# Keys kept on chip, three output products moved into the attention's order, and row sums taken later, in one step of a hybrid decoder

## The chip, the cores and the metric

The kernel runs on one core of a Trainium2 chip. A core has a matrix engine (TensorE, PE in the profile, with its weight loads as PEld), a vector engine (VectorE, DVE), an activation engine (ScalarE, ACT), a general engine (GpSimd, POOL) and a queue engine (SyncE, SP) that issues transfers. SBUF is the on-chip memory, PSUM the eight banks into which TensorE accumulates, and DRAM the memory off the core. The metric is the device time of one execution in microseconds, the median of three runs.

## The reference

One decoder layer is computed for 1024 prompt rows and for 8 sequences with 4 new rows each, 1056 rows in all, with the same weights and a model width of 1024:

```python
h = rmsnorm(x, g_norm1) * (1 + scale1) + shift1
za, zq, zkv, zg, zm = split(h @ w_in)
u, v = split(gelu(za)); ya = chunk_spatial_gating(u, layernorm(v), w_spatial, b_spatial)
yb = nsa_attention(q, kv_rows, win_rows, ...)     # compressed + selected blocks + window, gated
gate_a, gate_b = split(sigmoid(zm))
x = x + gate1 * ((gate_a * (ya @ w_branch_a) + gate_b * (yb @ w_branch_b)) @ w_out)
up = (rmsnorm(x, g_norm2) * (1 + scale2) + shift2) @ w_up
a, gv = split(causal_conv(up)); x = x + gate2 * ((gelu(a) * gv) @ w_down)
y = rmsnorm(x, g_final)
```

The prompt attends to its own 16 blocks of 64 keys and to a window of 512. The 8 sequences have 8192 past rows in a paged cache: all pages are read once for the compressed keys, and once more for the selected-block branch, in which blocks that were not selected are masked. The keys of the new rows are an output too.

## The kernel before

All activations lie with features on the 128 partitions and the 1056 rows along the free axis. A matrix product in float32 is made of three products: every operand x is split into hi (rounded to the type fp32r, by ScalarE) and lo (the rest, by VectorE), and hi*hi, hi*lo and lo*hi are summed in PSUM (split, L319 and L320; products, L415). Rows are taken in three chunks, 384, 384 and 288 wide (CH). Wide tiles of 1056 come from one pool of 24 slots (slot).

The order of the instructions on an engine is found by a planner at build time, which simulates the program with its own costs and takes what is ready, the earliest written first. A tile's memory is taken when its first user is planned and given back after its last. With issue_after, a program edge keeps one instruction behind another on its engine; the argument behind of products and of down is a list of (step, instruction): from that step on, the matmuls stay behind that instruction. In the attention stage the order of TensorE alone is written by hand (manual_schedule); the other engines are still planned.

The stages that the change touches, in order:

*The dense stage.* A list fill (L813) holds 22 dense products of h with w_in: four queries, two keys, sixteen merge gates, each stored to DRAM when done. Between them lie the compressions of the paged cache (compress, compress_act, compress_end), one per half sequence; the last two, n = 14 and 15, come after fill. key(j) (L731) evacuates one key head pair, copies the new rows' part and stores the rest to the output o_k. hh and hl, the split h, hold 16 of the 24 slots until the last dense product is through.

*Key tiles and queries.* key_tiles(j) (L837) loads a key tile back from o_k and makes four tiles: hi and lo for each of two heads, with the 64 partitions of the head copied to the other 64 as well. queries (L854) splits the queries of one tile of 128 rows; the queries are loaded back from DRAM (L871).

*Attention.* There are 32 units (8 tiles of 128 prompt rows, taken in the order 4, 5, 1, 6, 0, 7, 2, 3, by 4 heads of a group). step(n) makes the scores of unit n, turns the probabilities of unit n - 1 and multiplies the values of unit n - 2. Among these it deals out 32 paged steps (sel_step) that read the pages of the 8 sequences, 2 MB each, through a ring of four buffers (page_buffer), which the modulation weights, the sequences' window and at the end ya and w_ba use too. due tells before which unit how many paged steps should be done; it goes by work, the keys that a unit sees plus a constant:

```python
work = [i + 1 + min(i + 1, 5) + 6 for i, _ in units]
```

Chains of small operations (masks, the merge of paged steps) are generators in a list pending: each call of one_more counts down their waits and runs what is due, and a yield of k says that the next part comes k calls later. blocks(gr, bank) (L749) is such a chain: it makes the compressed branch and the block mask of four sequences. After the last unit, the remaining ones run one after the other.

*Branch outputs.* The eight outputs of ya @ w_branch_a are made after the attention's PSUM banks were given back, each in three chunks with a gate tile that is loaded from DRAM (L1355) and multiplied in when the bank is evacuated (L1358). Then come those of w_branch_b (L1368 loads the weights), w_out, and the up-projection.

*Down-projection.* Per chunk, eight outputs m of 22 steps each; the residual is added (residual), the squares of x are summed over m (squares, L1422), and at the chunk's end rstd_rows (L274) sums over the partitions with matmuls of one column (m1 is the last), makes the reciprocal root with small operations, and broadcasts it back with transposes (m2 is the last). Both are placed within the next chunk's products by behind. y_tile then scales the outputs and stores them.

## Time and profile before

| | |
|---|---|
| median of 3 runs | 1963.92 us (1961.31 to 1966.83) |
| the profiled execution's own time | 1964.85 us |
| its span, first to last instruction | 1963.0 us |
| mean granted TensorE clock | 0.977 |
| TensorE busy | 1847.5 us, 94% |
| VectorE, ScalarE, GpSimd busy | 60%, 40%, 24% |

Times are in us from the start of the span. In the groups, a row reads: line, engine, operation, out<-in with shapes, count, busy time, mean of one, and the idle time before them with what ended it. In a timeline a row begins with its start and its length; a last bracket holds the idle time before it and what ended it. SPq is the SP queue's own issuing. A matmul's end is modelled. A granted clock of 1.00 is TensorE's full clock. The stages lie thus: dense products until about 587, compressions 14 and 15 until about 602, attention from 609 to 1011, the w_branch_a products to about 1061, the rest of the mixer and the up-projection after it, and the down-projection from about 1716 on; the last row sums are at 1946.

### The profile page before, as it was taken

Reading aid. Unit: us, or ns where it says so; the run is one execution under the profiler, and the core shown is the slowest. Engines: PE = TensorE matmul, PEld = TensorE weight load, DVE = VectorE, ACT = ScalarE, POOL = GpSimd, SP = SyncE. Lnnn points to the kernel's source line nnn. Section 1 sums busy time; section 2 is a strip of 40 time slices with the busy share of each in tenths; the row PEclk is TensorE's granted clock in tenths of the full one; section 3 lists DMA queues with packets and bytes.
Section 4 is the critical chain, followed back from the end, with each engine's and each line's share of the span. In section 5 each row is a group of like instructions: output and inputs, shape, how many; then the busy total and the mean of one; then the engine's idle time right before and its main releaser. Section 6 shows DMA issues by size and latency. Waiting matters only on the chain.

```text
span 1963.0 us, 43697 instructions
## 1 busy us (share of the span) xinstructions
PE 1847.5 (94%) x16031; PEld 1740.0 (89%) x16031; DVE 1178.8 (60%) x2554; ACT 785.6 (40%) x1602; POOL 465.8 (24%) x613
## 2 busy tenths in 40 slices
PE   5899999999997998989989999899999999999996
PEld 3799999999996776757679998899999999999996
DVE  7615311111116666666665778989999999756464
ACT  4313111122114554646642356434444444545342
POOL 2410100100000000000001411567867675201010
PEclk9899999999998999989999999999999999999998
DMA  8445657775748677777774454233322223956462
GB/s 329 152 153 165 203 163 227 242 225 184 227 164 274 191 223 236 226 236 220 235 251 152 140 165 152 71 105 105 109 88 73 83 78 95 309 180 207 136 190 88
DMA packets 253893, 346.13 MB, mean 176 GB/s; under 512 B 35280, under 2 KB 189296, under 8 KB 251504
## 3 DMA queue, kind: packets, MB, share of 16 engines
q1 hardware_dynamic: 205696, 262.91, 42.5%
q10 hardware_dynamic: 36896, 41.22, 6.7%
q0 software_dynamic: 11088, 39.21, 5.6%
q8 instruction: 127, 2.08, 0.4%
q14 instruction: 86, 0.70, 0.1%
HBM read 305.96 MB, written 41.43 MB: 177 GB/s over the span
## 4 chain that ended last, share of the span: by engine, by line
PE 77%; DVE 6%; SPq 5%; DMA 5%; issue 3%; ACT 2%; DVEq 0%; ACTq 0%
PE t L56 75%; SPq L522 4%; DMA t<-w_ada 2%; PE t L1161 2%; DVE t L320 1%; DMA t<-t 1%; SPq L512 1%; ACT t L319 1%; DVE t L1135 1%; DMA t<-psel 1%; ACT t L1136 1%; ACT t L1165 1%; DMA t<-pcmp 0%; DVE t L338 0%; DMA t<-w_rows 0%
## 5 line engine op out<-in xcount | busy, mean ns | idle before, releaser
L56 PE MATMUL t<-t,t 128*128 128x264 f32 (+11 forms) x15256 | 1772.7, 305 | 84.7 <-DVE t L173 14.8
L56 PEld LDWEIGHTS t<-t,t 128*128 128x128 f32 (+2 forms) x15096 | 1658.6, 170 | 137.8 <-issue 61.6
L320 DVE TENSOR_TENSOR t<-t,t 128x512 fp32r<-128x512 f32 (+2 forms) x478 | 390.7, 825 | 317.7 <-ACT t L319 295.7
L319 ACT CAST t<-t 128x512 fp32r<-128x512 f32 (+5 forms) x544 | 310.5, 588 | 422.8 <-PE t L56 322.2
L1584 DVE TENSOR_TENSOR t<-t,t 128x264 f32<-128x264 f32 (+2 forms) x366 | 107.4, 339 | 12.8 <-PE t L56 12.8
L1192 POOL COPY t<-t 128x256 f32<-128x256 f32 x32 | 13.2, 412 | 298.9 <-DVE t L1190 190.8
L1161 PEld LDWEIGHTS t<-t,t 128*128 128x128 f32 x528 | 57.3, 142 | 29.2 <-ACT t L1010 9.2
L1521 ACT ACTIVATE t<-t,t 128x1072 f32<-128x1072 f32 x44 | 56.6, 1286 | 64.8 <-DVE t L1584 39.8
L1522 DVE SCALAR_TENSOR_TENSOR t<-t,t,t 128x1072 f32<-128x1072 f32 x44 | 71.6, 1627 | 10.7 <-ACT t L1521 10.1
L683 ACT ACTIVATE t<-t 128x384 f32<-128x384 f32 (+1 forms) x48 | 22.2, 465 | 138.6 <-PE t L56 89.1
L1136 ACT ACTIVATE t<-t,t 128x640 f32<-128x640 f32 (+3 forms) x64 | 56.2, 879 | 48.0 <-DVE t L1135 42.0
L1165 ACT COPY t<-t 128x512 f32<-128x512 f32 (+1 forms) x112 | 58.6, 567 | 40.4 <-PE t L1161 40.3
L1161 PE MATMUL t<-t,t 128*128 128x128 f32 x528 | 73.6, 278 | 0.7 <-DVE t L1213 0.3
L1135 DVE TENSOR_REDUCE t<-t 128x1 f32<-128x640 f32 (+3 forms) x64 | 58.9, 922 | 19.9 <-PE t L56 18.2
L1713 POOL TENSOR_TENSOR t<-t,t 128x384 f32<-128x384 f32 (+1 forms) x12 | 14.9, 1274 | 229.3 <-ACT t L1771 229.3
L1523 DVE SCALAR_TENSOR_TENSOR t<-t,t,t 128x1072 f32<-128x1072 f32 x44 | 63.2, 1435 | 0.0
L685 POOL DMA_DIRECT2D t<-t x16 | 8.5, 534 | 219.7 <-DVE t L684 165.0
L1547 POOL TENSOR_TENSOR t<-t,t 128x512 f32<-128x512 f32 x21 | 35.4, 1687 | 105.0 <-DMA t<-w_up 67.3
L1615 POOL TENSOR_TENSOR t<-t,t 128x1024 f32<-128x1024 f32 x22 | 54.3, 2469 | 17.1 <-ACT t L1614 17.1
L981 DVE TENSOR_TENSOR t<-t,t 128x512 f32<-128x512 f32 x32 | 22.1, 690 | 41.2 <-PE t L56 41.0
L1402 POOL TENSOR_TENSOR t<-t,t 128x384 f32<-128x384 f32 (+1 forms) x24 | 27.9, 1168 | 71.8 <-DVE t L1401 68.6
L320 DVE TENSOR_TENSOR t<-t 128x384 fp32r<-128x384 f32 (+1 forms) x66 | 36.2, 576 | 13.3 <-ACT t L319 13.2
(285 smaller groups left out, 1272.3 us busy)
## 6 DMA issues: line engine op xcount, KB each, us to landing
t<-psel SPq DMA_DIRECT2D x512, 128.0 KB
t<-pcmp SPq DMA_DIRECT2D x332, 128.0 KB
t<-w_down SPq DMA_DIRECT2D x120, 256.0 KB
t<-t POOLq DMA_DIRECT2D x50, 528.0 KB, 4.3
t<-w_up SPq DMA_DIRECT2D x96, 256.0 KB
t<-pcmp ACTq DMA_DIRECT2D x180, 128.0 KB
t<-w_ada SPq DMA_DIRECT2D x16, 1024.0 KB
t<-w_t ACTq DMA_DIRECT2D x52, 256.0 KB
```

What stands on the lines that cost most here:

```text
L56: return pe.matmul(out, lhsT, rhs, start=start, stop=stop)
L319: act.copy(hi, t)
L320: dve.tensor_tensor(lo, t, hi.bitcast(F32), op=OP.subtract)
L522: d = queue.dma_start(dst, src[bass.ds(r, 1)].rearrange("g p c -> p (g c)"))
L1135: dve.tensor_reduce(m4[:, branch, h:h + 1], ps[:, :, 0:w], axis=AX.XY, op=OP.max, negate=True)
L1136: act.activation(P[:, 0:L].rearrange("p (a c) -> p a c", a=2), ps[:, :, 0:w], AF.Exp, bias=m4[:, branch, h:h + 1], accum_out=s4[:, branch, ...
L1161: pe.transpose(pt[:, c:c + 128], probs[branch, h][:, 128 * b:128 * b + 128], ident)
L1165: (act.copy if w > 2 else dve.tensor_copy)(probs[branch, h][:, 128 * k:128 * (k + w)], pt[:, c:c + 128 * w])
L1521: act.activation(acc[:, 0:w], up[:, 0:w], AF.Identity, scale=cw[:, n, 0:1], bias=cw[:, n, 3:4])
L1522: dve.scalar_tensor_tensor(acc[:, 0:w], up[:, 1:1 + w], cw[:, n, 1:2], acc[:, 0:w], op0=OP.mult, op1=OP.add)
L1523: dve.scalar_tensor_tensor(acc[:, 0:w], up[:, 2:2 + w], cw[:, n, 2:3], acc[:, 0:w], op0=OP.mult, op1=OP.add)
L1584: dve.tensor_tensor(o, by4(banks[c][:, c0:c0 + n], n), other(c, c0, n) if other else o, op=OP.add)
```

## The change

- Both keys go to the end of fill, and key keeps its tile in kr_of. key_tiles reads this tile in place of loading o_k, and is called ahead of the query loads. The copy of k to the other 64 partitions is made by ScalarE from the key itself, not by VectorE from the rounded one. The queries of the first tile are split between compressions 14 and 15.
- In blocks the second yield is 6, not 3.
- The constant in work is 1, not 6.
- The loop body of the w_branch_a outputs becomes branch_a(m, bank). Outputs 0, 1 and 2 run inside the hand-written order, with the attention's banks (pM), and three calls of one_more after each chunk; outputs 3 to 7 run where all eight ran. products gets the argument bank.
- In the down-projection, m1 is asked for at step 12 of the next chunk's first output, not 4, and m2 at step 2 of its second output, not step 14 of the first.
- In the last chunk the last square isn't added to the sum by VectorE; the row sums take both tiles.

```diff
-    def products(w, xh, xl, a, b, evac, behind=()):
-        ps = pA()[:, 0:b - a]
+    def products(w, xh, xl, a, b, evac, behind=(), bank=pA):
+        ps = bank()[:, 0:b - a]
...
+    kr_of = []
     def key(j):
         kr = slot()
+        kr_of.append(kr)
...
-        yield 3
+        yield 6
         pt = bank()
...
-    fill = [lambda j=j: query(j) for j in range(4)] + [lambda j=j: key(j) for j in range(2)]
-    fill += [lambda j=j: merge_gate(j, slot()) for j in range(16)]
+    fill = [lambda j=j: query(j) for j in range(4)] + [lambda j=j: merge_gate(j, slot()) for j in range(16)]
+    fill += [lambda j=j: key(j) for j in range(2)]
...
-    def key_tiles(j, anchor):
+    def key_tiles(j):
...
-        kr = slot()
-        if anchor is not None:
-            dve.tensor_copy(kr[0:1, 0:1], anchor[0:1, R - 1:R])
-        sync.dma_start(kr[:, 0:NP], A["o_k"][j][:, 0:NP])
-        f = kr[:, 0:NP]
+        f = kr_of[j][:, 0:NP]
         for h, k, l in ((0, k0, l0), (1, k1, l1)):
             own, other = slice(64 * h, 64 * h + 64), slice(64 - 64 * h, 128 - 64 * h)
             act.copy(k[own, 0:NP], f[own])
+            act.copy(k[other, 0:NP], f[own])
             dve.tensor_tensor(l[own, 0:NP], f[own], k[own, 0:NP].bitcast(F32), op=OP.subtract)
-            dve.tensor_copy(k[other, 0:NP], k[own, 0:NP].bitcast(F32))
             dve.tensor_copy(l[other, 0:NP], l[own, 0:NP].bitcast(F32))
...
+    key_tiles(0)
+    key_tiles(1)
     qt = [slot() for _ in range(4)]
     for j in range(4):
         sync.dma_start(qt[j], q_d[j])
-    key_tiles(0, None)
-    key_tiles(1, None)
...
+    compress_act(*compress(14))
     q_first = queries(TILES[0], KL[0][0])
-    for n in (14, 15):
-        compress_act(*compress(n))
+    compress_act(*compress(15))
     compress_end()
...
-    work = [i + 1 + min(i + 1, 5) + 6 for i, _ in units]
+    work = [i + 1 + min(i + 1, 5) + 1 for i, _ in units]
...
         for n in range(len(units) + AHEAD):
             step(n)
+        ma = []
+
+        def branch_a(m, bank):
+            w = slot(F32R)
+            split(wba[:, m], w[:, 0:512], w[:, 512:1024])
+            w = [[w[:, c + 128 * k:c + 128 * k + 128] for k in range(4)] for c in (0, 512)]
+            t = slot()
+            dve.tensor_copy(t[0:1, 0:1], al[3].bitcast(F32)[0:1, R - 1:R])
+            sync.dma_start(t, sig_d[m])
+            for a, b in CH:
+                products(w, ah, al, a, b,
+                         lambda a, b, ps, t=t: dve.tensor_tensor(t[:, a:b], t[:, a:b], ps, op=OP.mult), bank=bank)
+                for _ in range(3):
+                    one_more()
+            ma.append(t)
+
+        for m in range(3):
+            branch_a(m, pM)
         while pending:
             one_more()
...
-    for m in range(8):
...
-        ma.append(t)
+    for m in range(3, 8):
+        branch_a(m, pA)
...
-                down(m, ff[n], banks[m], 0, 22, () if not done else ((4, m1), (14, m2)) if m == 0 else ((0, m2),))
+                down(m, ff[n], banks[m], 0, 22, () if not done else ((12, m1),) if m == 0 else ((2, m2),))
...
-                acc = squares(acc, x1[i][:, a:b], a, b)
+                if n == 2 and i == 7:
+                    sq = N2([128, 384], F32, "sq", 2)[:, 0:b - a]
+                    act.activation(sq, x1[i][:, a:b], AF.Square)
+                else:
+                    acc = squares(acc, x1[i][:, a:b], a, b)
...
-        pr, m1, m2 = rstd_rows(acc, a, b)
+        if n < 2:
+            pr, m1, m2 = rstd_rows(acc, a, b)
+        else:
+            pv = pT()
+            row_sums(pv, [acc, sq])
+            pr = rstd_rows(None, a, b, pv)[0]
```

More of the change, by code (lines that the diff above doesn't have):

```diff
@@ L1347, in step_kernel @@
     yh, yl = [], []
-    ma = []
-    for m in range(8):
-        w = slot(F32R)
-        split(wba[:, m], w[:, 0:512], w[:, 512:1024])
-        w = [[w[:, c + 128 * k:c + 128 * k + 128] for k in range(4)] for c in (0, 512)]
-        t = slot()
-        dve.tensor_copy(t[0:1, 0:1], al[3].bitcast(F32)[0:1, R - 1:R])
-        sync.dma_start(t, sig_d[m])
-        for a, b in CH:
-            products(w, ah, al, a, b,
-                     lambda a, b, ps, t=t: dve.tensor_tensor(t[:, a:b], t[:, a:b], ps, op=OP.mult))
-        ma.append(t)
+    for m in range(3, 8):
+        branch_a(m, pA)
     R3S.release()
```

## The prediction

> **What bounds the kernel now.** I read the page first, then the waits of TensorE stage by stage, then the timeline around its longest waits, and last the windows there for the granted clock.
>
> ```profile
> PE 1847.5 (94%) x16031; PEld 1740.0 (89%) x16031; DVE 1178.8 (60%) x2554; ACT 785.6 (40%) x1602; POOL 465.8 (24%) x613
> ```
>
> TensorE is busy for 94% of the span and no other engine for more than 60%. No part of the change takes a large product away, so what it can win is the time in which TensorE stands still, or runs at a lower clock after it stood still. I go through these places one by one. The profiled execution took 1964.85 us, a span of 1963.0 and 1.85 around it; the median of the runs is 1963.92, 0.93 less. The terms are taken from the profiled time, and the result is then set against the median.
>
> **Part A, the keys stay in SBUF.** The next rows are from the timeline of all engines between the last dense product and the first attention score.
>
> ```profile
> 585.48 1.09 SPq L843 DMA_DIRECT2D t<-o_k  x2
> ...
> 586.93 14.51 PEld L56 LDWEIGHTS t<-t,t 128*64 128x64 f32 x272 [0.16 <-PE t L56]
> ...
> 593.26 2.11 ACT L847 CAST t<-t 64x1024 fp32r<-64x1024 f32 x2 [5.81 <-DMA t<-o_k]
> 594.34 1.22 DVE L848 TENSOR_TENSOR t<-t,t 64x1024 fp32r<-64x1024 f32 x1 [5.65 <-ACT t L847]
> ...
> 597.72 2.22 ACT L864 CAST t<-t 64x128 fp32r<-64x128 f32 x7
> 598.28 1.41 DVE L850 CAST t<-t 64x1024 fp32r<-64x1024 f32 x2
> ...
> 602.57 0.57 PE L56 MATMUL t<-t,t 128*64 128x64 f32 x8 [0.89 <-ACT t L553]
> ...
> 608.39 0.29 DVE L569 TENSOR_TENSOR t<-t,t 64x128 f32<-64x128 f32 x1
> 608.80 1.03 PEld L56 LDWEIGHTS t<-t,t 128*128 128x128 f32 x4 [5.79 <-issue]
> 608.83 6.10 PE L56 MATMUL t<-t,t 128*128 128x320 f32 x24 [5.69 <-DVE t L569]
> ```
>
> From 586.93 TensorE has compressions 14 and 15 to do, until about 601.4, and this is the cover for making the key tiles. The keys come back from o_k only at 593.26, and then VectorE has four of L848 (1.22), and eight copies of 1.41/2 = 0.7 (L849 and L850): 10.5 us in its queue, and L568 and L569 of the last compression stand behind them. They end at 608.68, and the first score goes at 608.83.
>
> After: the loads of o_k go. The last key's evacuation takes the place of the last merge gate's, so key tiles can begin when the slots of hh and hl come free in the last dense chunk, near 585 to 587. ScalarE gets eight casts of 2.11/2 = 1.05, 8.4 us, until about 595.5; VectorE keeps four of 1.22 and four of 0.7, 7.7 us, a step behind. The query loads (L871) move behind the key tiles and start some 5 us later; if they need the 7.8 us that the first o_k load took behind them (issued 585.48, read at 593.26), they land near 595, and eight L864 of 0.3 us end near 598. All this is done before 601.4. What is late next is the last compression's own end: the eight matmuls at 602.57, 0.57, then L568 and L569 of about 0.3 each on VectorE, so the first score can go at about 603.9. That is 4.9 us earlier.
>
> The windows give the clock after such a wait (length, then busy time and count of PE, PEld, DVE, ACT and POOL, granted clock, DMA share, GB/s).
>
> ```profile
> 604.70:614.90 10.20, 6.07 (x24) 5.13 (x24) 6.26 (x18) 1.51 (x3) 0.00 (x0) 0.50 0.95 258
> 628.40:632.00 3.60, 3.60 (x53) 2.79 (x55) 1.80 (x6) 0.86 (x4) 0.40 (x1) 0.53 0.69 194
> 785.67:802.49 16.82, 16.04 (x202) 12.76 (x202) 14.60 (x46) 12.61 (x32) 0.85 (x2) 1.00 0.71 207
> 802.49:815.25 12.76, 11.91 (x147) 9.66 (x146) 7.57 (x16) 8.01 (x19) 0.92 (x3) 1.00 0.67 201
> 1011.00:1014.30 3.30, 3.30 (x11) 3.30 (x12) 1.65 (x9) 0.00 (x0) 0.00 (x0) 0.50 1.01 403
> 1778.90:1782.30 3.40, 3.40 (x13) 3.40 (x13) 2.27 (x8) 3.19 (x8) 0.00 (x0) 0.50 0.91 300
> ```
>
> After 5.7 us of standing, 6.07 us of matmuls ran at half clock, a loss of up to 3.0. About 2 us of standing remain, and by the second row that too brings a short half-clock stretch, so I count only 0.6 of it. Term A: 5.5, between 0 (the new copies end no sooner) and 7.9. The key stores and the eight small o_wsk stores move from before the merge gates to this place on POOL's queue, ten issues; nobody waits for them but the slots' next users, so I count nothing. If they held a slot back, A's lower bound takes it in.
>
> [...]
>
> **Part B, the mask of the second group.** In the waits of TensorE from 600 to 1070:
>
> ```profile
> PE t L56 <- DMA t<-psel: 7.3, 5, 1.8
> ...
> PE t L56 <- DVE t L789: 2.0, 1, 2.0
> ```
>
> L789 is the end of the mask's chain on VectorE; with three more calls between, TensorE has the next scores and the values of unit 0 to do meanwhile. After that wait the clock was 0.53 for 3.6 us of full work (row 628.40), up to 1.7 lost. B: 2.5, between 0 and 3.7. If scores can't fill it, a bank's evacuation is late next (that is why I don't take all).
>
> [...]
>
> **Part C, fewer paged steps in small tiles.** With 1 in place of 6 in the work of a unit, paged steps 3, 7, 8, 16, 24 and 25 move one unit earlier; units 4, 7, 15 and 23 (large tiles) get two, and units 5, 9, 16 and 25 one less. The number of matmuls is the same. A unit of tile 6 with two steps lasted 16.82 and the next, with one, 12.76, both at full clock and 0.93 to 0.95 busy, so doubling a large unit costs nothing beside the 4.1 us of the step itself. But pages must be there. The timeline of the SP queue and the source line of its page loads show how they come.
>
> ```profile
> 630.18 7.06 SPq L522 DMA_DIRECT2D t<-psel  x11
> 649.81 1.43 SPq L1053 DMA_DIRECT2D t<-w_ada  x2
> 651.85 25.27 SPq L522 DMA_DIRECT2D t<-psel  x35
> ```
>
> ```profile
> L522 SPq DMA_DIRECT2D t<-psel x464: 332/333/2155, 651.9 to 987.8; - x155
> ```
>
> SP issues 464 loads, 29 steps of 16, in 335.9 us, or 11.6 us a step, with hardly a break; before that it stood from 637 to 650 because all four page buffers were in use. So the pages, not TensorE, set the pace in places (7.3 us of waits on psel). But what starts the long run of issues at 651.85 is a buffer that TensorE frees, and A and B bring that forward by 8; step 3's buffer is now the one of the window stage, freed a little before. So the shift goes through to the end of attention. On top of it the psel waits can shrink: C is 1.5, a fifth of 7.3, since pages run only about 2 us further ahead; between +7.3 and -7.3 (the same again, if steps wait for pages that come at the old pace).
>
> **Part D, three w_ba outputs in the attention's order.** TensorE at the end of attention, and VectorE after it:
>
> ```profile
> 1004.77 1.48 PE L56 MATMUL t<-t,t 128*64 128x128 f32 x24
> 1006.68 0.35 PE L56 MATMUL t<-t,t 128*128 128x1 f32 x2 [0.44 <-DVE t L1030]
> 1010.97 1.41 PE L56 MATMUL t<-t,t 128*128 128x32 f32 x4 [3.93 <-DVE t L1040]
> ```
>
> ```profile
> 1017.42 0.69 DVE L320 TENSOR_TENSOR t<-t,t 128x512 fp32r<-128x512 f32 x1 [4.01 <-ACT t L319]
> 1018.03 0.55 DVE L1358 TENSOR_TENSOR t<-t,t 128x384 f32<-128x384 f32 x1
> ```
>
> The last merge of the paged branch is a chain of small operations with nothing between; TensorE waits 0.44 and 3.93, and then runs 3.30 us at clock 0.50 (row 1011.00), 1.6 lost. Nine chunks of 12 matmuls now lie there, about 2 us each, with three calls after each, so the merge's two last steps come after a chunk or two. The splits of their operands lie in the two steps before (ya_split in step), so they should be there when TensorE is through with the last values at 1004.77 + 1.48 = 1006.3; if not, D's lower bound takes it in. The evacuations are what is late next: the first was made at 1018.03, behind a split that waited for w_bb. Earlier chunks put the evacuations ahead of it in the plan; the gate loads have the whole DMA there (share 1.01 in row 1011.00), and four banks hold four chunks, 7.4 us. D: 5.0 of 6.0, between 0 and 6.0.
>
> **Part E, the row sums further back.** In the down-projection, between chunks 0 and 1:
>
> ```profile
> 1770.76 4.15 PE L56 MATMUL t<-t,t 128*128 128x384 f32 x23
> 1778.19 1.68 PE L56 MATMUL t<-t,t 128*128 128x1 f32 x8 [3.28 <-DVE t L1430]
> ```
>
> ```profile
> PE t L56 <- DVE t L1430: 5.6, 3, 3.3
> ```
>
> TensorE did 4 of 22 steps of the next output and stood 3.28 for the last sum of squares, then ran 3.40 at clock 0.50 (row 1778.90), 1.7 lost. Eight steps more are 24 matmuls of 4.15/23 = 0.18 or less, some 4 us, which covers the 3.28. The broadcast (m2) keeps 12 steps between, 10 before, so its chain has no less cover. The other chunk boundary has 5.6 - 3.3 - 1.9 = 0.4 of the same wait. Together 5.4; the products need weights that VectorE splits in time, so E is 4.5, between 0 and 5.4. The output scaling behind it comes later by 3 to 4 us and keeps the VectorE work that now delays the splits; it is only moved.
>
> **Part F, the last sum of squares.** The end of the kernel:
>
> ```profile
> 1945.38 0.46 DVE L1430 TENSOR_TENSOR t<-t,t 128x288 f32<-128x288 f32 x1 [0.51 <-ACT t L1429]
> 1945.89 0.93 PEld L56 LDWEIGHTS t<-t,t 128*128 128x128 f32 x6 [2.10 <-DVE t L1430]
> 1945.90 1.01 PE L56 MATMUL t<-t,t 128*128 128x1 f32 x6 [1.87 <-DVE t L1430]
> ```
>
> One addition goes (0.46 and its hand-over, 0.5), and TensorE sums two tiles: 12 records in place of 6 in 1.01. If those of the first tile run early, 0.5 is won; if they alternate, four more of 0.17 cost 0.7 and 0.2 is lost. I take 0.
>
> The sum: A 5.5 + B 2.5 + C 1.5 + D 5.0 + E 4.5 + F 0 = 19.0. From 1964.85 that gives 1945.9; beside the median, 1963.92 - 19.0 = 1944.9, so 1945.
>
> **The rivals.**
>
> *One cover fails.* Either the evacuations of the w_ba chunks stay behind the w_bb split (until 1017.42, as now), and D is lost: four banks filled from 1006.3 last until 1013.7, so the wait of 3.9 only moves; 1950. For it speaks the order of the rows above, against it that chunks done earlier are planned earlier. Or the slots delay the key tiles so that L569 still ends near 608.7: A lost, 1950.5. For it: they must wait for the last dense chunk; against: 586.93 to 601.4 is 14.5 us for 8.4.
>
> *The page loads set the end of attention.* If the 11.6 us a step hold from an unchanged 651.85, A, B and C are swallowed there: 9.5 lost, 1954.4. For it: SP is never idle after 651.85. Against: that start hangs on a buffer that TensorE frees.
>
> *Slower: the moved steps outrun their pages.* Place: units 4, 7, 8, 15, 23 and 24. Six steps are wanted a unit (12.8 us by row 802.49) earlier, while pages come at 11.6 a step. If half of each, 6.4, stays a wait that later units don't give back, that is 38.4 against 17.5 won elsewhere (the sum without C): 1963.9 + 20.9 = 1985. It makes the kernel slower (by over 0.3%, 5.9 us) once 23.4 are not given back, 3.9 a step. Against it: waits with four buffers let the loads run on, so later steps find their pages.
>
> *The change does not do what it says:* the plan of the other engines shifts, and new small waits eat what is won: 1964.
>
> **How the numbers follow.** All five waits mostly gone: 0.62, own range 1938 to 1951. One cover fails: 0.17. Pages set the end: 0.11. Slower by the pages: 0.05. Nothing: 0.05. A difference under 0.3% (5.9 us) can't be told from none by such a measurement. Faster: 0.62 + 0.17 + most of 0.11 = 0.88; same 0.07; slower 0.05. The low end of the range is the sum with all terms but C at their upper bounds and C at twice its value (7.9 + 3.7 + 3.0 + 6.0 + 5.4 + 0.5 = 26.5, 1937.4); the high end takes in the rival of the pages with some loss, 1957.
>
> **What would show it.** A: no wait on o_k; the first 128x320 score follows the 128*64 matmuls by about 1.5 us. B: no wait on the mask line. C: the page loads' long run begins near 641 and has no longer breaks; psel waits under 7.3 in sum. D: no 3.9 us wait before the last 128x32, and no wait for a w_ba evacuation in its place. E: the 128x1 row sums start without a wait. F: under 0.5 either way. I am wrong if the waits on psel or on exp of paged steps grow, or if TensorE waits for banks at the end of attention.

## The result and the profile after

The kernel after took 1948.82 us (median of 4 runs, 1944.34 to 1950.22) against 1964.43 for the kernel before in the same comparison (4 runs, 1961.31 to 1966.83). The ratio is 0.9918, with a 95% interval of 0.9896 to 0.9939: 15.6 us won, between 12.0 and 20.4. 1945 was forecast, with 19.0 us won. The profiled execution took 1950.22 us, a span of 1948.2, at a mean granted clock of 0.982 (before: 0.977). Some us of such a number are luck, as will be seen: a second profiled execution of the same kernel took 1944.72.

The first part of the page of after shows that the same work was done: TensorE is busy 3.4 us less, so most of what was won is standing time.

```profile
PE 1844.1 (95%) x16037; PEld 1734.9 (89%) x16037; DVE 1177.1 (60%) x2549; ACT 790.5 (41%) x1606; POOL 468.6 (24%) x613
```

**Ahead of the attention.** The timeline of after, all engines, between the last dense product and the first score (start, length, what; in the bracket the idle time before and what ended it):

```profile
585.36 1.05 ACT L847 CAST t<-t 64x1024 fp32r<-64x1024 f32 x1
...
592.07 1.04 ACT L847 CAST t<-t 64x1024 fp32r<-64x1024 f32 x1
592.37 1.22 DVE L848 TENSOR_TENSOR t<-t,t 64x1024 fp32r<-64x1024 f32 x1
593.80 0.77 DVE L849 CAST t<-t 64x1024 fp32r<-64x1024 f32 x1
...
594.58 2.39 DVE L864 TENSOR_TENSOR t<-t,t 64x128 fp32r<-64x128 f32 x8
...
602.38 0.57 PE L56 MATMUL t<-t,t 128*64 128x64 f32 x8 [0.63 <-ACT t L553]
602.99 0.28 DVE L568 TENSOR_SCALAR t<-t,t 128x64 f32<-128x64 f32 x1 [5.53 <-PE t L56]
603.29 0.29 DVE L569 TENSOR_TENSOR t<-t,t 64x128 f32<-64x128 f32 x1
603.73 2.48 PE L56 MATMUL t<-t,t 128*128 128x320 f32 x16 [0.77 <-DVE t L569]
```

Nothing loads o_k any more. The key tiles begin at 585.36 and are through at 594.6, the first queries at 597.0, and VectorE has stood for 5.53 us when the last compression asks for L568. The first score goes at 603.73, 5.10 earlier, after 0.63 + 0.77 us of standing where 0.89 + 5.69 stood.

**The end of the attention.** TensorE and VectorE of after:

```profile
1001.74 6.27 PE L56 MATMUL t<-t,t 128*128 128x384 f32 x38
1009.71 4.50 PE L56 MATMUL t<-t,t 128*128 128x32 f32 x25 [1.70 <-DVE t L1039]
```

```profile
1004.39 0.56 DVE L1342 TENSOR_TENSOR t<-t,t 128x384 f32<-128x384 f32 x1
...
1007.56 0.35 DVE L1039 SCALAR_TENSOR_TENSOR t<-t,t,t 128x128 f32<-128x128 f32 x1
1008.05 0.46 DVE L1342 TENSOR_TENSOR t<-t,t 128x288 f32<-128x288 f32 x1
1008.42 0.35 DVE L1039 SCALAR_TENSOR_TENSOR t<-t,t,t 128x128 f32<-128x128 f32 x1
1008.70 0.69 DVE L320 TENSOR_TENSOR t<-t,t 128x512 fp32r<-128x512 f32 x1
1009.31 0.35 DVE L1039 SCALAR_TENSOR_TENSOR t<-t,t,t 128x128 f32<-128x128 f32 x1
```

The w_ba chunks (128x384) run where TensorE stood 3.93 us, and their evacuations (L1342) come from 1004.39 on, not behind the split for w_bb. 1.70 us of standing are left, because an evacuation and a split stand between the three steps of the merge's L1039.

**The rest.** The waits of TensorE in the down-projection, of after:

```profile
PE t L56 <- ACT t L319: 2.4, 1, 2.4
PE t L294 <- DVE t L305: 2.1, 2, 1.6
PE t L56 <- ACT t L1770: 1.3, 1, 1.3
PE t L56 <- DVE t L320: 0.9, 1, 0.9
```

The 5.6 us for the addition of squares are gone; 0.5 came at the broadcast of the first boundary (the other 1.6 of L305 is the end of the kernel, as before) and 1.26 for the last square.

The windows after these places give the clock (length; busy time and count of PE, PEld, DVE, ACT and POOL; granted clock; DMA share; GB/s):

```profile
603.60:606.20 2.60, 2.47 (x18) 2.14 (x18) 1.27 (x3) 0.52 (x2) 0.00 (x0) 1.00 1.01 379
1009.60:1014.30 4.70, 4.59 (x27) 4.60 (x28) 2.94 (x12) 1.66 (x3) 0.00 (x0) 1.00 0.96 338
1705.30:1708.90 3.60, 3.60 (x14) 3.60 (x13) 3.36 (x7) 2.56 (x6) 0.00 (x0) 0.53 1.04 387
1776.80:1783.00 6.20, 6.16 (x37) 6.16 (x38) 6.20 (x7) 3.07 (x7) 5.01 (x5) 1.00 0.58 191
```

The half clock after the first score, after the merge and at the first chunk boundary is gone. One at 1705.30 is new, at the start of the down-projection, after the 2.4 us for L319; the kernel before stood 2.21 us at that place and kept full clock (1.00 from 1714.78 to 1718.19).

**And in the attention something was lost.** From the first values of unit 0 to the last unit's (the transpositions at L1200, L1201 before) the two kernels took, in windows of before and of after:

```profile
630.66:1002.90 372.24, 339.82 (x4052) 261.35 (x4052) 245.14 (x648) 214.09 (x570) 27.98 (x71) 0.98 0.72 226
```

```profile
620.52:998.46 377.94, 343.25 (x4092) 263.52 (x4092) 245.55 (x654) 215.25 (x572) 27.79 (x71) 0.97 0.74 229
```

A lead of 10.1 us at the first values is 4.4 at the last. The waits for page rows grew from 7.3 to 10.2, and those for the exponentials of paged steps (L983 and L984) too; these rows are from the waits of TensorE from 600 to 1070, of before and of after:

```profile
PE t L991 <- ACT t L984: 10.9, 10, 2.5
```

```profile
PE t L990 <- ACT t L983: 12.0, 13, 2.5
PE t L56 <- DMA t<-psel: 10.2, 4, 4.1
```

Those were the signs that the prediction had named for being wrong, so the experiments began with part C.

The page loads show how much of the lead reached the end. SyncE had issued 48 of them, three steps, by 637 in the kernel before and then stood until 650; in after it issues four steps without such a break:

```profile
607.29 43.37 SPq L522 DMA_DIRECT2D t<-psel  x64
```

The last load was issued at 980.1, 7.7 us earlier than in before (987.8). TensorE's last wait for page rows ended 4.1 us behind that (984.2; before 2.4, 990.2), and the last values came 18.4 us behind it (before 15.1).

### The profile page after: what moved, and what is told of

Read it like the earlier page. It is cut to its first block, busy times and chain, and to the rows that moved or that the text cites. A ratio compares the mean times of both kernels' runs of the same rounds, so it can differ in the third digit from the quotient of the medians.

```text
span 1948.2 us, 43689 instructions
## 1 busy us (share of the span) xinstructions
PE 1844.1 (95%) x16037; PEld 1734.9 (89%) x16037; DVE 1177.1 (60%) x2549; ACT 790.5 (41%) x1606; POOL 468.6 (24%) x613
## 4 chain that ended last, share of the span: by engine, by line
PE 78%; DVE 6%; DMA 4%; issue 4%; SPq 4%; ACT 3%; POOL 1%; DVEq 0%; ACTq 0%; POOLq 0%
PE t L56 75%; SPq L522 3%; PE t L1160 2%; DMA t<-w_ada 2%; DVE t L320 1%; DMA t<-t 1%; DMA t<-psel 1%; DVE t L1591 1%; PE t L990 1%; DVE t L1529 1%; DMA t<-xT 1%; DVE t L1530 1%; DVE t L1134 0%; ACT t L1135 0%; SPq L512 0%
## 5 line engine op out<-in xcount | busy, mean ns | idle before, releaser
L56 PE MATMUL t<-t,t 128*128 128x264 f32 (+12 forms) x15262 | 1766.4, 304 | 72.1 <-DVE t L173 14.8
L319 ACT CAST t<-t 128x512 fp32r<-128x512 f32 (+5 forms) x544 | 311.1, 589 | 413.0 <-PE t L56 313.5
L1591 DVE TENSOR_TENSOR t<-t,t 128x264 f32<-128x264 f32 (+2 forms) x366 | 106.9, 338 | 11.4 <-PE t L56 11.4
L1135 ACT ACTIVATE t<-t,t 128x640 f32<-128x640 f32 (+3 forms) x64 | 56.1, 877 | 41.3 <-DVE t L1134 36.4
L1720 POOL TENSOR_TENSOR t<-t,t 128x384 f32<-128x384 f32 (+1 forms) x12 | 13.9, 1190 | 225.9 <-ACT t L1787 225.9
L1622 POOL TENSOR_TENSOR t<-t,t 128x1024 f32<-128x1024 f32 x22 | 54.3, 2468 | 16.3 <-ACT t L1621 16.3
```

The lines of the kernel that those rows point to most:

```text
L56: return pe.matmul(out, lhsT, rhs, start=start, stop=stop)
L319: act.copy(hi, t)
L1135: act.activation(P[:, 0:L].rearrange("p (a c) -> p a c", a=2), ps[:, :, 0:w], AF.Exp, bias=m4[:, branch, h:h + 1], accum_out=s4[:, branch, ...
L1591: dve.tensor_tensor(o, by4(banks[c][:, c0:c0 + n], n), other(c, c0, n) if other else o, op=OP.add)
```

## The experiments

All kernels are compared by the same stages: the first 128x320 score of TensorE; its first values; the last unit's values; the start of w_bb (VectorE's write that anchors yl); the end of the last row sum; the end of the span. Differences between these, in us:

| kernel | first score | first values | to last values | to w_bb | to last row sum | to the end |
|---|---|---|---|---|---|---|
| before | 608.83 | 630.66 | 372.2 | 58.2 | 885.6 | 16.3 |
| after | 603.73 | 620.52 | 377.9 | 54.0 | 879.7 | 16.1 |
| after_again | 601.05 | 617.77 | 376.4 | 54.0 | 878.5 | 16.0 |
| e1_const6 | 603.63 | 620.22 | 370.5 | 55.6 | 886.7 | 15.9 |
| e2_pages_two_queues | 604.70 | 625.12 | 376.8 | 54.0 | 880.1 | 16.2 |
| e3_ada_pool | 604.40 | 621.00 | 370.3 | 55.6 | 884.1 | 10.6 |
| e4_two_calls | 604.33 | 620.92 | 376.3 | 52.1 | 880.7 | 15.9 |
| e5_const6_two_calls | 603.51 | 620.09 | 380.0 | 52.1 | 878.2 | 16.2 |
| e6_three_edits | 602.79 | 619.38 | 376.2 | 52.1 | 881.1 | 10.9 |
| e7_const1_alone | 607.11 | 628.90 | 381.8 | 58.2 | 882.3 | 16.2 |
| e8_const7_two_calls | 602.68 | 619.25 | 375.2 | 52.1 | 880.7 | 15.8 |
| e9_const1_two_calls | 601.58 | 618.16 | 375.8 | 52.1 | 882.0 | 16.2 |
| e10_without_outputs_and_sums | 603.74 | 620.33 | 379.3 | 58.9 | 884.0 | 15.9 |
| e11_without_keys_and_yield | 605.34 | 628.49 | 373.9 | 54.1 | 875.9 | 16.1 |

**The constant back at 6.** In the kernel after:

```diff
-    work = [i + 1 + min(i + 1, 5) + 1 for i, _ in units]
+    work = [i + 1 + min(i + 1, 5) + 6 for i, _ in units]
```

> The changed kernel with the constant in work back at 6. In the changed kernel TensorE was 10.1 us ahead of the kernel before at the values of unit 0 and 4.4 us ahead at the values of unit 30. Theory P (the issue of pages on the SP queue sets the end of attention, whatever the order of the steps): the values of unit 30 come within 2 us of the changed kernel's 993.2, the last wait on psel stays near 4 us, and the time is within 3 us of the changed kernel's. Theory S (the steps that stand two to a unit outrun their pages, and that is what gave the lead back): the waits on psel fall from 10.2 us to 7 or less, the values of unit 30 come 4 to 6 us earlier, near 988, and the time falls by as much.

Median 1950.57 (1947.14 to 1956.89, 5 runs), ratio to before 0.9945 (0.9923 to 0.9966): no faster than after. In the one profiled execution the last unit's values started at 990.73, 7.7 us ahead of after, but from w_bb to the last row sum it took 886.7 us where after took 879.7. I read this first as two facts: the constant 1 costs 7.7 us, and something later takes them back. The first reading fell, as e5, e8 and e9 show below.

**Pages through two queues.** A quarter of the page loads goes to ScalarE's queue:

```diff
-                   after, (), 3)
+                   after, (3, 7), 3)
```

> The changed kernel with every fourth group of four page loads issued on ScalarE's queue in place of SP's. Theory P (SP's issue rate, 9.7 us for 16 loads, sets the pace): SP needs 7.3 us a step, psel waits fall from 10.2 us to under 3, the values of unit 30 come 4 us or more earlier (near 988), the time falls by 3 to 6 us. Theory S: the pages were late only for where the steps stand; the loads come no sooner in the places that count, and exps behind the issues on ScalarE make it the same or up to 4 us slower. If neither queue but the DMA engines are the limit, psel waits stay and the time is the same.

Median 1958.49 (10 runs), ratio 0.9964 (0.9947 to 0.9982), worse than after. The waits of TensorE from 600 to 1070 show why:

```profile
PE t L990 <- ACT t L983: 15.2, 17, 2.5
PE t L56 <- ACT t L1135: 5.7, 8, 1.8
PE t L56 <- DVE t L991: 5.4, 7, 1.1
```

No wait for page rows is left, of 10.2, and still the attention took 376.8: about half of what the pages no longer cost, waits for ScalarE's exponentials cost (12.0 to 15.2 at L990, and 3.7 to 5.7 at L1135); that this is because the same engine now issues loads between them is likely, but not shown. Besides, the first values came 4.6 us later than in after: a half-clock stretch of 10.24 us followed the first score here. So "faster pages" is not a gain by itself.

**The late w_ada loads on GpSimd's queue.**

```diff
-            sync.dma_start(st[:, p0:p0 + 2048], A["w_ada"][ch][:, p0:p0 + 2048])
+            pool.dma_start(st[:, p0:p0 + 2048], A["w_ada"][ch][:, p0:p0 + 2048])
```

> The changed kernel with the late modulation weights (eight times 2 MB) loaded from GpSimd's queue in place of SP's. Theory P: SP loses some 1 us of issuing and up to 3 us of standing behind a full queue per 2 MB, seven times after the first; the last page load is issued 5 to 15 us sooner, the waits on psel fall below 5 us, and the values of unit 30 come 3 to 6 us earlier. If the DMA engines are the limit, the page loads only wait there, and nothing moves by more than 2 us. Theory S: no change over 2 us.

One run: 1943.39. 5.3 us of waits for page rows, a short attention (370.3), a long stretch behind w_bb (884.1), as in e1, and some 5.4 us less at the very end, which neither theory had in it; more on that in the last section. What theory P says SyncE loses is near what the trace of after has: two issues of w_ada take 0.85 us, and of the 11 waits before a page load that ended with a landing of w_ada (19.1 us in all) the longest is 3.1; that a full queue is behind them was an assumption, which no run shows. The last page was issued 3.8 us sooner than in after, less than theory P's 5 to 15, and the last values came 7.2 us earlier, more than its 3 to 6 and than theory S's 2.

**Two calls per chunk.** One call of one_more less after each w_ba chunk inside the attention's order:

```diff
-                for _ in range(3):
+                for _ in range(2):
```

> The changed kernel with two calls of one_more after each w_ba chunk in place of three, which puts the last matmul of the paged branch's merge a chunk later. If the 1.7 us wait before it (it stands behind evacuations and splits on VectorE) is only a matter of its place, the wait goes, and the time from the values of unit 31 to the first w_bb product falls by 1.5 us or so; if VectorE is late altogether, the wait moves to the chunk behind and nothing is won.

One run: 1947.48. The 1.70 us of standing at the merge are gone; TensorE's timeline has one unbroken row there, and the stage takes 52.1 us, 1.9 less:

```profile
1001.83 10.42 PE L56 MATMUL t<-t,t 128*128 128x384 f32 x65
```

**Constant 6 with two calls.** e1 and e4 together. The planner writes the orders of VectorE, ScalarE and GpSimd anew for every edit, and in the up-projection, 200 us behind the edit, that of e1_const6 differs from that of after at 76 of the first 330 instructions of VectorE. With two calls it differs at 13.

> The kernel after, with the work constant back at 6 (as in e1_const6) and two calls of one_more per chunk of w_ba instead of three (as in e4_two_calls). Theory O (planner's order): what e1_const6 won in the attention it lost again in the up stage because the planner, fed with another attention, wrote another order for VectorE there (76 of its first 330 instructions stand elsewhere than in the kernel after). In this kernel only 13 of 330 do. O expects the last unit's values at 990 to 992, the start of w_bb near 1044.5 (1046.3 of e1_const6 less the 1.9 of the two calls), from there to the last row sum 879 to 882 (after: 879.7; e1_const6: 886.7), a span of 1940 to 1942 and a median of 1940 to 1944. Rival L (the stages behind the attention take the lead back whatever the order, by loads or by chance of the clock): 885 to 888 from the start of w_bb to the last row sum, a span of 1946 to 1949, a median of 1947 to 1951.

Median 1945.49 (1939.01 to 1948.28, 6 runs), ratio 0.9890 (0.9868 to 0.9911). From w_bb to the last row sum: 878.2, a little under theory O's 879 to 882 and far from rival L's 885 to 888. But the last unit's values came at 1000.04, not at 990 to 992: the attention took 380.0, though e1 and e5 are the same program as far as w_ba. The windows, of e1 and of e5:

```profile
620.22:990.73 370.51, 339.92 (x4092) 261.65 (x4092) 246.24 (x654) 214.87 (x572) 27.98 (x71) 0.98 0.75 234
```

```profile
620.09:1000.04 379.95, 344.82 (x4093) 263.43 (x4092) 246.74 (x655) 215.05 (x571) 27.88 (x71) 0.96 0.73 228
```

Of the 9.4 us, 4.9 are TensorE busy for longer at a lower clock (0.96 for 0.98) and 4.5 are more standing. Both go with the page loads. Here are all loads of psel on SyncE's queue (shortest, middle and longest issue in ns; first and last start) and TensorE's last wait for page rows, of e1 and of e5:

```profile
L522 SPq DMA_DIRECT2D t<-psel x512: 332/333/1698, 606.3 to 975.8; - x171
978.08 1.29 PE L56 MATMUL t<-t,t 128*32 128x512 f32 x8 [1.22 <-DMA t<-psel]
```

```profile
L522 SPq DMA_DIRECT2D t<-psel x512: 332/333/1920, 606.6 to 985.1; - x171
987.39 1.29 PE L56 MATMUL t<-t,t 128*32 128x512 f32 x8 [1.87 <-DMA t<-psel]
```

The last load is issued 9.3 us later in e5, and in both the wait ends 2.3 us and the last values come 15.0 us behind it. From the 65th load on SyncE waited for TensorE for 1.9 us in either, so it wasn't TensorE that held the loads up; why they were slower in e5 stays open.

One program, on two chips, differs by more than what I had put down to the constant from a pair of traces. Theory O is borne out in the stage it spoke of. Its starting point in the attention is not, the span (1946.5) is rival L's, and the median lies 1.5 us above O's bounds and as far below L's, so by itself it decides nothing.

Theory O has one more witness. The longest wait for an evacuation of the up-projection (L1591) is 5.1 in both kernels with the other order (e1 and e3), 2.5 in after, 3.4 in e5; waits of TensorE from 1190 to 1360, of after, e1 and e3:

```profile
PE t L56 <- DVE t L1591: 5.2, 4, 2.5
```

```profile
PE t L56 <- DVE t L1591: 10.1, 7, 5.1
```

```profile
PE t L56 <- DVE t L1591: 10.2, 6, 5.1
```

The sum alone doesn't tell them apart (e5 has 9.5), but of the eleven traces with the new row sums, e1 and e3 alone need over 882.0 us behind w_bb (886.7 and 884.1, against 875.9 to 882.0 in the nine others). So a planner's order that VectorE got through an edit elsewhere seems to cost some 5 us. It rests on two traces, and no run changed that order alone.

**All three edits together.** Constant 6, w_ada on GpSimd's queue, two calls.

> As e5_const6_two_calls, and the late loads of w_ada issued by the GpSimd queue instead of SyncE's (as in e3_ada_pool, where the last page was issued 3.8 us earlier). VectorE's order in the up stage differs from that of the kernel after at 19 of 330, as in e4_two_calls. Theory G (pages still hold the attention's end at constant 6: TensorE waited 7.0 us for them in e1_const6): the waits for page rows fall below 5 us, the last unit's values start at 985 to 988, median 1936 to 1940. Rival T (at constant 6 the attention is bound by TensorE's own work and the two engines beside it): the last unit's values at 989 to 992 as in e1_const6, median equal to that of e5_const6_two_calls within 2 us.

Median 1942.79 (1939.60 to 1949.82, 6 runs), ratio 0.9891 (0.9868 to 0.9915): the lowest median of all, 6 us under after, though the intervals of the two ratios overlap, so it isn't shown to be faster; nor than e5, whose ratio is 0.9890. The waits for page rows were 11.5 us, and the last values came at 995.53. Theory G (under 5 us, 985 to 988) fell, and T's bounds were missed too, for the last values (989 to 992) and for the median (2.7 below e5's, not within 2). What e6 has over e5 at a fixed place, by one trace of each, is the 5.3 us at the end.

**Constant 1 alone.** In the kernel before:

```diff
-    work = [i + 1 + min(i + 1, 5) + 6 for i, _ in units]
+    work = [i + 1 + min(i + 1, 5) + 1 for i, _ in units]
```

> The kernel before with the work constant at 1 and nothing else. Theory S (the constant alone moved the paged steps ahead of their pages): as in after against e1_const6, 7.7 us: the last unit's values at 1008 to 1012 (before: 1002.9), the waits for page rows at 10 or more (before: 7.3), span 1968 to 1972, median 1969 to 1973 against 1964.3. Rival K (it is the keys' edit that hurt, because it starts the page loads 1.8 us later and puts the queries' loads behind it, and the constant is harmless): the last unit's values at 1002 to 1004 and a median of 1963 to 1966.

Median 1968.80 (10 runs) against 1965.44, ratio 1.0018 (1.0001 to 1.0036). By its trace, theory S held but for the span (last values at 1010.70, page waits 16.0; span 1967.4, 0.6 short), by its median it falls just below S's bounds and 2.8 above K's: 3.4 us slower, with anything from 0.2 to 7.1 possible, and the planner's order behind the attention isn't that of before either (20 of 320 instructions of VectorE).

**After, once more.** No edit.

> The kernel after, unchanged, for a second trace. If the places of the half-clock stretches are chance: some of those of the first trace (756.5, 848.6, 855.5, 985.2 in the attention; 1200.2, 1241.2, 1265.1, 1705.4 later) are gone or have moved, and the last unit's values start within 3.5 us of 998.5. If they hang on the place alone: the same list, each within 1 us after its wait.

1944.72. The last values start 4.3 us earlier than in the first trace, more than the 3.5 expected of chance, 2.7 of it there at the first score already. Half-clock stretches in the attention began at 751.2 (13.65 us long), 833.1, 898.0 and 979.9; counted from the first score, those of the first trace at 152.8 and 381.5 us are there again within 2.6 us (150.2 and 378.9), the other two moved or are new. Behind the attention the same four places came again, counted from w_bb's start within 2.5 us, one of them half as long. So neither expectation held alone: in these two traces four places behind the attention and two in it kept their stretch, one at half its length, and the other two in the attention moved or are new.

**The constant alone, with the same order behind it.** With two calls, constants 7 and 1 give the same instructions in the same order on every engine from the attention's last unit on.

```diff
-    work = [i + 1 + min(i + 1, 5) + 1 for i, _ in units]
+    work = [i + 1 + min(i + 1, 5) + 7 for i, _ in units]
```

> The kernel of e9_const1_two_calls with the work constant at 7 instead of 1. From the last unit of the attention on, the two have the same instructions in the same order on every engine (the two before, with 1 and 6, had not); constants 6 and 7 deal out the same but for one paged step at one unit. So the pair shows the constant alone. Theory S (the constant 1 moved steps ahead of their pages, 7.7 us between the first traces of the kernels with 1 and 6): median 6 to 9 us below that of e9_const1_two_calls, about 1939, and the stretch from the first score to the last unit's values 386 to 389 us against 393 to 395. Theory N (the attention's length differs by some 5 us between executions of one program: e1_const6 and e5_const6_two_calls are the same program up to w_ba, and took 387.1 and 396.5 from the first score to the last unit's values; the constant is worth less than 3 us): medians equal within 3 us, the stretch anywhere from 387 to 397.

> The kernel of e4_two_calls again, on the same chip as e8_const7_two_calls. Theory S: median 1946 to 1949, 6 to 9 above e8_const7_two_calls, the waits for page rows at 8 to 12 us against 5 to 7. Theory N: median within 3 us of e8_const7_two_calls; the waits for page rows between 4 and 13 us in both, without order.

Constant 7: 1947.97 (1944.65 to 1951.02, 6 runs), ratio 0.9909 (0.9889 to 0.9930). Constant 1: 1946.54 (1945.43 to 1948.24, 5 runs), 0.9903 (0.9881 to 0.9924). Medians within 1.4 us, the wrong way round for theory S, which wanted 1 to be 6 to 9 slower; attentions of 375.2 and 375.8. Theory N stands. The waits of TensorE from 600 to 1070, of e8 and of e9, show what the constant does change and what differs without it:

```profile
PE t L56 <- DMA t<-psel: 10.1, 4, 4.1
PE t L990 <- ACT t L983: 9.0, 10, 2.2
PE t L56 <- ACT t L1135: 5.8, 13, 1.0
```

```profile
PE t L990 <- ACT t L983: 12.0, 13, 2.5
PE t L56 <- DMA t<-psel: 5.7, 3, 2.1
PE t L56 <- ACT t L1135: 3.7, 9, 0.7
```

Waits for page rows lie between 4.9 (e4) and 16.0 (e7) with constant 1, and between 7.0 (e1) and 12.5 (e5) with 6 or 7. Those for the exponentials at L990 (L991 in before, e7 and e11) do follow it: 11.5 to 12.2 with 1, 8.5 to 10.9 with 6 or 7 (e2, with its ScalarE issues, left out), and L1135 goes the other way by 1 to 2.

**A, B and C without D, E and F**, and **C to F without A and B**. The first is the kernel after with these lines as before, and the last square added as before:

```diff
-        for m in range(3):
-            branch_a(m, pM)
...
-    for m in range(3, 8):
-        branch_a(m, pA)
+    for m in range(8):
...
-                down(m, ff[n], banks[m], 0, 22, () if not done else ((12, m1),) if m == 0 else ((2, m2),))
+                down(m, ff[n], banks[m], 0, 22, () if not done else ((4, m1), (14, m2)) if m == 0 else ((0, m2),))
```

> The kernel after without its parts D, E and F: all eight w_ba outputs stand behind the attention again, the row sums of a chunk stand where they stood in the kernel before, the last square is added as before; the keys, the yield and the constant stay. VectorE's order in the up stage is that of both kernels. Theory M (what is won ahead of the attention stays to the end): over the traces so far the first unit's values start at 620 with the keys' edit and at 630 without, so the median falls by 8 to 11, to 1954 to 1957; the prediction's terms for the keys, the yield and the constant give 9.5, 1955. The waits of 3.9 at the start of w_bb and of 3.3 (2.9 in a second trace) before the row sums in the down-projection are back. Rival P (the page loads set the end of the attention, so the lead is gone there): 1961 to 1966.

Median 1959.87 (9 runs), ratio 0.9964 (0.9948 to 0.9980), 7.1 us under before, between 3.9 and 10.2. The first values came at 620.33 as asked, and the waits of 3.93 at the merge and 2.56 at the first row sums were back:

```profile
1007.61 4.61 PE L56 MATMUL t<-t,t 128*128 128x32 f32 x14 [3.93 <-DVE t L1039]
```

```profile
1774.82 5.49 PE L56 MATMUL t<-t,t 128*128 128x1 f32 x32 [2.56 <-DVE t L1429]
```

The median lies between theory M's bounds (2.9 above 1957) and rival P's (1.1 below 1961), nearer to P's. The ratio's interval excludes that the whole lead is lost, and holds the 9.6 or so that M expects; some of the lead may be lost.

The second undoes, in the kernel after, the keys' edit and the yield:

```diff
-        yield 6
+        yield 3
...
-        f = kr_of[j][:, 0:NP]
+        kr = slot()
...
+        sync.dma_start(kr[:, 0:NP], A["o_k"][j][:, 0:NP])
+        f = kr[:, 0:NP]
```

> The kernel after without its parts A and B: keys through o_k and the mask's yield as before; constant 1, the three w_ba outputs in the attention, the row sums and the last square as after. VectorE's order in the up stage differs at 10 of 320 from that of both. Theory M (the parts add up): the three waits gone give 4.2 + 3.3 + 0.5 = 8.0 from the first pair of traces, the constant 0: 1955 to 1959; the prediction's terms give 5.0 + 4.5 + 0 + 1.5 = 11, 1953.6. Rival C (the constant costs what e7_const1_alone showed over before, 3.4 with 0.2 to 7.1): 1958 to 1963. A trace with the wait before the first row sums of the down-projection still there, or the start of w_bb still behind it by more than 2 us, is against both.

Median 1958.29 (12 runs), ratio 0.9968 (0.9955 to 0.9981), 6.3 us under before, between 3.7 and 8.8. Theory M (1955 to 1959) and rival C (1958 to 1963) both hold that median; the three waits are gone as M asked, with 1.70 left at the merge. Its profiled execution, 1950.43, was the fastest of its twelve, 7.9 below their median: a trace shows which waits are there, not what a kernel takes.

The parts add up within their errors: 7.1 + 6.3 = 13.4 for the two halves (the constant counted in both), 15.6 for the whole.

## Why the prediction was right, point by point

The mean over the traces with a part less the mean without it gives each term a second measurement, steadier than one pair: first values 619.8 (ten traces, e2 left out) against 629.4 (three); w_bb's start 54.0 behind the last values against 58.2 to 58.9; the stretch to the last row sum 879.6 (nine, e1 and e3 left out) against 884.0 (three). That is 9.6 + 4.2 + 4.3 = 18.1 us. The attention itself, in means further down, gives back 1.7, which leaves 16.4, where the sum was 19.0 and the medians differ by 15.6 (12.0 to 20.4). With e1 and e3 in, the last term is 3.3 and not 4.3.

- **A, the keys (5.5), and B, the yield (2.5).** The order of events was that of the prediction: first score forecast for 603.9, measured 603.73; queries done by 598, measured 597.0; the last compression's own end late next. B's wait on L789 (2.0) is gone, but 1.5 us of standing came at 626.12 for nothing that the profile shows. It is there in all eleven traces with the edit and in none of the three without, and it stands behind the first values, so the 9.6 measured there doesn't have it: 8.1 with it, where 8.0 were forecast. That the two agree is partly luck, since two steps were off in opposite ways: B's cover was taken as better than it is, and A's clock was too small: "about 2 us of standing remain, and by the second row that too brings a short half-clock stretch, so I count only 0.6 of it". 1.40 us remained, no half clock followed (1.00 in the row 603.60), and most of the 3.0 was won; in e2 it did follow the same 1.4 us, for 10.24 us.
- **C, the constant (1.5).** This step failed in its reasoning: "the psel waits can shrink: C is 1.5, a fifth of 7.3, since pages run only about 2 us further ahead". They didn't shrink, and hardly could be seen to do anything, since with SyncE alone issuing the pages they lie anywhere between 5 and 16 us. What moved steadily were the exponentials' waits, 1 to 3 us more, with 1 to 2 less at L1135. Mean length of the attention: 376.5 with 1 (eight traces, e2 left out), 374.8 with 6 or 7 (five), in a spread of 370 to 382 either way. So C is somewhere between -2 and nothing, inside its bounds of -7.3 to +7.3. Its heaviest rival, moved steps that outrun their pages by 38 us, did not come about in any trace. The rival of the pages was half right: in all thirteen traces with the pages on SyncE's queue alone, TensorE's last wait for page rows ended 2.3 to 4.1 us behind the issue of the last load, and the last values came 15.0 to 18.4 us behind it, so the pages do hold the end of the attention. What it had wrong is that their long run would start no earlier. The prediction's "So the shift goes through to the end of attention" held: SyncE's break after the first 48 loads was 14.9, 12.4 and 12.3 us without A and B, and at most 4.3 with them, and the last load was issued at 987 to 996 without them and at 976 to 985 with them. How much of the lead is then kept differs from run to run (e10).
- **D, three outputs (5.0).** 4.2 (55.6 in e1 and e3; in e3 the clock was 0.58 from 1005 to 1008). The wait moved less than it should: 1.70 remain, behind what the prediction named as late next, evacuations and a split between the merge's steps, though not those for w_bb. The 1.6 of half clock were won. Two calls instead of three win the rest, 1.9 (e4, and the 52.1 of e5, e6, e8 and e9).
- **E, the row sums (4.5).** In the first pair of traces, start of the down-projection to the last square, 3.4 (230.1 to 226.7), with a half-clock stretch at its start that before didn't have; over the traces, with F and the up-projection in it, 4.3, or 3.3 with e1 and e3. The step "eight steps more ... covers the 3.28" held in all eleven traces with it; what is left is a wait of 0 to 1.3 at the broadcast.
- **F, the last square (0).** From its start to the division by its sum (L286) 2.04 us became 1.58. The upper bound, 0.5, was the better guess: the row sums of the first tile run early.
- **A sign that was no good.** "I am wrong if the waits on psel or on exp of paged steps grow": both grew in the first trace, and the total came out as forecast. The exponentials' did so in every trace with the constant 1, but by too little to be seen in the total. A sign must be one that two executions of a program agree on. The waits on o_k, on the mask, at the merge and on the row sums are of that kind (gone or there in every trace as the parts are), those on pages are not.

## What to carry to other kernels

A stretch of a kernel whose waits hang on many transfers can differ by 9 us between two executions of one program (here e1 and e5, 370.5 and 380.0); before a term is read off a pair of traces, run one of the two again, or compare against every trace that shares the stretch; and look when the last of the transfers was issued, since here the end of the stretch stood 15.0 to 18.4 us behind it in thirteen traces. When a planner writes the order, an edit also rewrites stages that it doesn't touch: compare the written orders first, and choose variants that share them behind the edit (here constants 1 and 7 with two calls), so that the difference is the edit's alone. Standing time that hangs on a fixed chain (a load back from DRAM, a chain of small operations, one column of row sums) is the sure kind of gain: each of these came within 2 us of what was read from its rows, the clock behind it included.

## What the runs showed of the hardware

**The end of the program waited for GpSimd.** In the view of the program's last line (L1871, where the engines meet; L1855 in before), each row has the shortest, the middle and the longest duration in ns. Of after and of e6:

```profile
L1871 POOLq DRAIN  x3: 40/107/12252, 1935.1 to 1947.9; - x3
L1871 SPq DRAIN  x3: 7/7/7, 1942.2 to 1947.6; - x3
```

```profile
L1871 POOLq DRAIN  x3: 40/107/3757, 1931.9 to 1939.0; - x3
L1871 SPq DRAIN  x3: 7/7/7, 1938.4 to 1938.7; - x3
```

The last packet of the output ends at 1941.0 in after and SyncE is through at 1942.2, but GpSimd's drain, begun at 1935.09, lasts 12.25 us, and the others leave behind it, 5.2 us later. It lasted 12.25 in the traces of before, after, after_again and e9, and 3.75 in those of e3 and e6, in which GpSimd also issues the 16 late loads of w_ada (before and after have 127 transfers on its queue, without these). By the table, the end came 15.8 to 16.3 us behind the last row sum in the twelve traces without these loads on GpSimd's queue, and 10.6 and 10.9 in the two with them. The transfers by queue, of after and of e3 (packets, MB, share):

```profile
q0 software_dynamic: 11088, 39.21, 5.7%
```

```profile
q0 software_dynamic: 13392, 55.99, 8.0%
```

So some 5.4 us went at the end with 16 transfers more on that queue. The last of GpSimd's transfers is issued at 1696.5 in after, some 240 us ahead of the drain. What in the count or the sizes goes with 12.25 or 3.75 wasn't tried and stays open.

**The clock after short waits.** In the traces of before and after there are 28 waits of TensorE of over 1.4 us between 600 and 1930. 20 of them overlapped a stretch at a granted clock of 0.50 or were followed by one within 1.4 us; 8 were not. The shortest that was is 1.65 us, in before; the longest that wasn't is 2.23, in after:

```profile
853.07 0.66 PE L991 MATMUL t<-t,t 128*128 128x128 f32 x4 [1.65 <-ACT t L984]
```

```profile
808.30 1.29 PE L56 MATMUL t<-t,t 128*32 128x512 f32 x8 [2.23 <-DMA t<-psel]
```

The windows behind these two waits, of before and of after:

```profile
853.07:856.48 3.41, 2.59 (x36) 1.80 (x36) 0.92 (x2) 1.21 (x2) 0.00 (x0) 0.62 0.66 198
```

```profile
808.30:811.71 3.41, 3.32 (x24) 1.95 (x24) 1.69 (x3) 1.44 (x3) 0.00 (x0) 1.00 0.99 408
```

The twelve half-clock stretches of before and the eight of after in that part of the span are 3.41, 6.83 or 10.24 us long. So in these traces the length of a short wait doesn't tell by itself whether it cost clock; what else decides wasn't tried.
